# The last 256 tokens of the last projection, turned: tokens in the partitions instead of output channels

## The chip, the core and the metric

The kernel runs on one core of a Trainium2 chip. A core has a matrix engine (PE, with its weight loads shown as PEld), a vector engine (DVE), a scalar engine (ACT), GpSimd (POOL), and SyncE (SP), which here issues the DMA transfers. Each engine works through its own queue in order; they meet through semaphores. The metric is the device time of one execution in microseconds (us), the median over several runs.

## The reference, cut to what matters

Two layers over 1024 tokens of 1024 channels: one of attention, one of a gated recurrence. Each adds its result, times a gate per channel, to the residual stream. At the end stands an RMS norm per token. All of it is float32.

```python
def rmsnorm(x, g):
    x32 = x.astype(jnp.float32)
    y = x32 * lax.rsqrt(jnp.mean(x32 * x32, axis=-1, keepdims=True) + EPS)
    return (y * g.astype(jnp.float32)).astype(x.dtype)

# in rglru_mixer, layer 1: hs are the states of the recurrence
    y = jnp.transpose(hs, (1, 0, 2)).astype(h.dtype) * jax.nn.silu(gate)
    return y @ w_out
# in reference
        x = x + gate[:, None, :] * y
    return rmsnorm(x, final_g)
```

The change concerns `y @ w_out`, the gated addition and the final norm, for the last 256 of the 1024 tokens.

## The kernel before

Everything is kept with channels in the 128 partitions and tokens in the free dimension; a tensor of 1024 channels is 8 tiles (KT). A float32 product is made of three matmuls on rounded halves: the high half of the weight with the high half of the data, low with high, high with low (`gemm`, line 324). So one output tile of 128 channels takes 8 x 3 matmuls. All engine calls go through one recording helper, so nearly every row of the profile has line 85; rows are told apart by the names of their tiles.

Layer 1 runs in slots, one for each of 8 channel tiles (`slot`, and `last_slots` for the last two). In a slot ACT makes the gates, DVE scans over the tokens (`hs`), and the result, gated, is split into a high and a low half, `y1h` and `y1l`. Three engines share the splitting: ACT writes the high half, POOL or DVE subtracts for the low one.

The weights of the last projection, `wo1`, come in 8 output tiles of two halves each (`raw_wo`, 256 KB each) through three buffers of the pool `wp`, and are split into `wout`. The tile of output channels 0 (`whi_wo`, `wlo_wo`) stays in the small rotating buffers; tiles 1 to 4 and 5 to 7 (`wo`, by `split_out`) go into large ones that held the input of the layer before. A raw buffer is loaded again only when its split is done.

The last projection (from line 1609) has three stages of tokens: 0 to 511, 512 to 767, and 768 to 1023. In each, PE makes 8 output tiles. Of the first four tiles of the first stage PE does the first seven of eight channel tiles ahead, since the last slot's states come late. `residual` (DVE) multiplies by the gate column `mod` and adds `x`, which was read back from DRAM (`x1d`); ACT squares, DVE adds the squares up in `sqa`. PE sums over the partitions with a column of ones (`psq_n`), DVE and ACT make the root, two or four transposes spread the factor over the partitions (`rs_n`), and DVE and POOL multiply (`end_norm`). These sums run while the next stage is already on PE: its steps are put between matmuls through the list `pending`.

Matmuls stay in the order in which they are written (`ordered` holds "pe" there). In layer 1 all engines do, up to the end of the first stage of the projection; from there on a scheduler places what is not on PE, and it may place such work before earlier calls of the same engine. The order that it made can be read from the built program.

Of the kernel before, what the change touches and what calls it, by code (L numbers as in the profile page):

```python
# [12 lines left out]
F32 = mybir.dt.float32  # L13
F32R = mybir.dt.float32r
AF = mybir.ActivationFunctionType
ALU = mybir.AluOpType
# [27 lines left out]
def r32(ap):  # L44
    return ap.bitcast(F32)
# [3 lines left out]
def hybrid_trunk(  # L49
# [17 lines left out]
    maskrow: bass.AP,  # L67
    sinks: bass.AP,
    b_f: bass.AP,
    outT: bass.AP,  # L70
):
    nc = tc.nc
    ordered = set()
# [37 lines left out]

    def sub(eng, out, a, b):
        eng.tensor_tensor(out=out, in0=a, in1=b, op=ALU.subtract)

    const = ctx.enter_context(tc.tile_pool(name="const", bufs=1))
    wp = ctx.enter_context(tc.tile_pool(name="wp", bufs=1))
# [1237 lines left out]
    wout, wr = [], []  # L1354

    def split_out(e, engs=(gp, gp), parts=(0, 1)):

        n = e - 1
        if n % 4 == 0 and 0 in parts:
            wr[:] = [hl.tile([P, 4, KT, P], F32R, tag=f"hl{n // 4 * 2 + i}", name=f"wo1_{e}_{i}") for i in range(2)]  # L1360
        for c in parts:
# [162 lines left out]
    def last_slots(c):  # L1524

        w = ready.popleft()
        ps = gates(c)
        gate_s(c - 1, 1)  # L1530
        r, i_ = sig_ri(c, ps)
        split_r(c + 1)
        gate_a(c - 1, 0)
        split_next()
        th, a_, a2 = rt("th", c), rt("a", c), rt("a2", c)
        act.activation(th, r, AF.Tanh, scale=sp[:, c : c + 1])
        mul(dve, i_, i_, xcs[c])
# [16 lines left out]
        split_next()  # L1554
        wout.append(ready.popleft())
# [40 lines left out]
    norms = []  # L1596

    def end_norm(xn, psq, t0, tw):
        h, o = t0 // HALF, t0 % HALF
        for e in range(KT):  # L1600
            act.activation(xn[:, e], xn[:, e], AF.Copy, scale=col[:, C_FG + e : C_FG + e + 1])
        rs, prs = rstd_of(psq, tw, xp, ("vb", "rsb"), f"n2_{t0}")()
        for e in range(KT):
            mul(*((gp, xn[:, e], xn[:, e], rs) if e % 4 == 3 else (dve, xn[:, e], xn[:, e], prs[:, :tw])))
            if e % 2:
                sync.dma_start(outT[:, h, e - 1 : e + 1, o : o + tw], xn[:, e - 1 : e + 1])

    for t0, tw in ((0, 512), (512, 256), (768, 256)):
        h, o = t0 // HALF, t0 % HALF
        ts = slice(t0, t0 + tw)  # L1610
        xn = xp.tile([P, KT, tw], F32, tag="xn", name=f"x2_{t0}")
# [4 lines left out]
        for e in range(KT):  # L1616
# [18 lines left out]
            for e_, w_, ps in late_:  # L1635
                if t0 == 0 and e_ < AHEAD:
                    gemm(ps[:, :tw], w_, y1h[:, :, ts], y1l[:, :, ts], range(last, KT), first=False)
                residual(xn[:, e_], ps[:, :tw], 1, e_)
                if t0 < 768 or e_ + 1 < KT:
                    square_sum(sqa, xn[:, e_], e_, xp, f"o1_{t0}")  # L1640
            late_ = []
        ordered.clear()
        ordered.add("pe")
        sqs = [sqa]
        if t0 == 768:
            sqs.append(xp.tile([P, tw], F32, tag="sq", name=f"sq7_{t0}", bufs=2))
            act.activation(sqs[1], xn[:, KT - 1], AF.Square)
        psq, steps = sum_steps(sqs, tw, f"n2_{t0}")
        norms.append((xn, psq, t0, tw, steps))
        if t0 < 768:  # L1650
            continue
        for f in steps:
            f()
        end_norm(*norms.pop()[:4])


def _buckets(n):
# [7 lines left out]
def layouts(inputs):  # L1665
# [10 lines left out]
    def colv(v):  # L1676
# [30 lines left out]
        "maskrow": mask,  # L1707
        "sinks": f["attn_sinks"][0],
        "b_f": f["attn_b_f"][0],
    }  # L1710
    return {k: np.ascontiguousarray(v) for k, v in arrays.items()}

# [17 lines left out]
```

## Time and profile before

| | us |
|---|---|
| median of 3 runs | 873.88 (873.17 to 874.44) |
| the profiled execution | 874.64 |
| its span, first to last instruction | 872.8 |
| last matmul of the projection ends | 862.04 |
| first store of the last stage is issued | 867.39 |

PE is busy 98% of the span at a mean granted clock of 0.992. Between the span and the time of the execution lie 1.84 us that the trace doesn't show. A profile is of one execution; durations in it are for one instruction from start to end, and instructions of one engine overlap a little, so what a row of instructions costs is read from the distance of their starts.

### The profile page before, as it was taken

To read this page: it belongs to the slowest core of one execution; us is meant where nothing else is said; L and a number is where in the kernel's file an instruction comes from. 1 tells how busy PE (TensorE), PEld (TensorE's weight loads), DVE (VectorE), ACT (ScalarE), POOL (GpSimd) and SP (SyncE) were. 2 spreads that over 40 slices of the span, in tenths; PEclk is the share of its full clock that TensorE was granted. 3 is DMA by queue.
4 is the path that set the end of the run, shared out by engine and by line. 5 is a ranking of instruction groups with operands and counts; after the bars stand their busy time and mean duration, and the time that the engine had idled before them with its cause. 6 is when DMAs were issued, how large, how long until landed. Compare 5 with 4: busy or idle time off the path is not lost.

```text
span 872.8 us, 13447 instructions
## 1 busy us (share of the span) xinstructions
PE 854.9 (98%) x4618; PEld 728.4 (83%) x4618; DVE 567.6 (65%) x1121; ACT 535.8 (61%) x1047; POOL 382.1 (44%) x418
## 2 busy tenths in 40 slices
PE   9999999999999999999999999999999999999995
PEld 8888798888888888888888888878888877787995
DVE  6876567688677466566665668466676555973644
ACT  5756124688776565566766657457678666964632
POOL 3843132333343232232475564633755566875001
PEclk8999999999999999999999999999999999999998
DMA  9943772100113223333364464421212112226042
GB/s 344 403 168 132 221 231 86 43 25 25 37 44 115 88 79 125 89 92 119 100 200 151 157 206 169 133 78 61 80 55 72 55 60 74 97 90 212 1 145 97
DMA packets 54620, 103.83 MB, mean 119 GB/s; under 512 B 6960, under 2 KB 20720, under 8 KB 54040
## 3 DMA queue, kind: packets, MB, share of 16 engines
q1 hardware_dynamic: 53400, 101.93, 35.3%
q10 hardware_dynamic: 1152, 1.05, 0.5%
q8 instruction: 36, 0.59, 0.3%
q14 instruction: 32, 0.26, 0.1%
HBM read 94.02 MB, written 8.93 MB: 118 GB/s over the span
## 4 chain that ended last, share of the span: by engine, by line
PE 81%; DVE 5%; POOL 5%; issue 4%; ACT 3%; DMA 1%; SPq 0%; DVEq 0%; POOLq 0%; ACTq 0%
PE ps_fill L85 23%; PE pst L85 10%; PE ps_o L85 8%; PE ps_lx L85 6%; PE ps_o0c L85 5%; PE ps_lg L85 5%; PE oB L85 4%; PE ptB L85 3%; PE sB L85 3%; PE ps_v L85 3%; PE sA L85 2%; PE oA L85 2%; PE ptA L85 1%; POOL wo L85 1%; POOL wlo_lx L85 1%
## 5 line engine op out<-in xcount | busy, mean ns | idle before, releaser
L85 DVE TENSOR_TENSOR ptl_B<-ptB,pth_B 128x512 fp32r<-128x512 f32 (+1 forms) x80 | 50.9, 636 | 44.2 <-ACT pth_B L85 43.7
L85 PE MATMUL ps_o<-y1h,wo 128*128 128x256 f32 (+1 forms) x336 | 76.2, 320 | 0.7 <-POOL wo L85 0.7
L85 ACT ACTIVATE pB<-pB,mnB 128x128 f32<-128x128 f32 (+3 forms) x64 | 49.6, 775 | 32.2 <-DVE mnB L85 31.5
L85 ACT ACTIVATE pth_B<-ptB 128x512 fp32r<-128x512 f32 (+1 forms) x80 | 44.0, 552 | 33.6 <-PE ptB L85 33.3
L85 DVE SCALAR_TENSOR_TENSOR xc_r<-ps_lx,col,xc_r 128x509 f32<-128x509 f32 (+2 forms) x48 | 35.6, 744 | 43.4 <-ACT xt_r L85 42.2
L85 PEld LDWEIGHTS ps_o<-y1h,wo 128*128 128x128 f32 x336 | 56.1, 190 | 5.4 <-POOL wo L85 1.1
L85 POOL TENSOR_SCALAR_AFFINE_SELECT pB<-pB 128x128 f32<-128x128 f32 x64 | 18.8, 295 | 94.7 <-DMA pB<-gd 82.2
L85 PE MATMUL pst<-hh,ws 128*128 128x512 f32 x192 | 55.4, 397 | 0.0
L85 PE MATMUL ps_o<-y1l,wo 128*128 128x256 f32 (+1 forms) x168 | 53.6, 319 | 0.0
L85 PE MATMUL ps_lg<-h1h,wlo_lg 128*128 128x512 f32 x128 | 50.2, 392 | 0.9 <-POOL wlo_lg L85 0.8
L85 PE MATMUL ps_lx<-h1l,whi_lx 128*128 128x512 f32 x128 | 50.3, 393 | 0.2 <-POOL h1l L85 0.2
L85 PE MATMUL ps_lx<-h1h,wlo_lx 128*128 128x512 f32 x128 | 50.3, 393 | 0.1
L85 PE MATMUL ps_lx<-h1h,whi_lx 128*128 128x512 f32 x128 | 50.3, 393 | 0.0
L85 PE MATMUL ps_lg<-h1l,whi_lg 128*128 128x512 f32 x128 | 49.9, 390 | 0.0
L85 PE MATMUL ps_lg<-h1h,whi_lg 128*128 128x512 f32 x128 | 49.9, 389 | 0.0
L85 POOL TENSOR_TENSOR wlo_lx<-raw_lx,whi_lx 128x512 fp32r<-128x512 f32 x16 | 30.6, 1929 | 43.3 <-ACT whi_lx L85 26.8
L85 ACT ACT_TABLE_LOAD x35 | 44.9, 1283 | 5.1 <-issue 3.0
L85 PE MATMUL ptB<-ident,pB 128*128 128x128 f32 x288 | 45.3, 273 | 2.1 <-ACT pB L85 1.6
L85 PEld LDWEIGHTS ptB<-ident,pB 128*128 128x128 f32 x288 | 35.7, 140 | 12.8 <-ACT pB L85 2.8
L85 DVE CUSTOM_DVE_ANT_0 pB<-sB,pB 128x384 f32<-128x384 f32 (+2 forms) x64 | 35.1, 553 | 14.6 <-PE sB L85 8.1
L85 PEld LDWEIGHTS pst<-hh,ws 128*128 128x128 f32 x192 | 36.1, 189 | 8.7 <-issue 0.6
L85 ACT ACTIVATE pA<-pA,mnA 128x256 f32<-128x256 f32 (+1 forms) x64 | 31.2, 488 | 10.8 <-DVE mnA L85 10.5
(313 smaller groups left out, 2827.7 us busy)
## 6 DMA issues: line engine op xcount, KB each, us to landing
ada<-in_ada_dram SPq DMA_DIRECT2D x32, 512.0 KB
x<-in_xT_dram SPq DMA_DIRECT2D x20, 256.0 KB
ada<-in_ada_dram SPq DMA_DIRECT2D x4, 1024.0 KB
pB<-gd SPq DMA_DIRECT2D x8, 512.0 KB
raw_o0a<-in_wo_dram SPq DMA_DIRECT2D x16, 256.0 KB
raw_o0c<-in_wo_dram SPq DMA_DIRECT2D x16, 256.0 KB
x1d<-x SPq DMA_DIRECT2D x16, 256.0 KB
raw_lx<-in_wl_dram SPq DMA_DIRECT2D x16, 256.0 KB
```

What stands on the lines that cost most here:

```text
L85: ins = issue(*args, **kw)
```

## The change

The first two stages stay as they are. For the last 256 tokens the roles of the two operands are exchanged: 128 tokens of the gated states are loaded as weights, and the projection's weights move, 512 output channels at a time. The result has tokens in the partitions. So:

- the sum of squares of a token lies along the free dimension: ACT sums while it squares (`accum_out`), and the norm factor is one number per partition, with no matmul of ones and no spreading;
- the gate and the final factor `final_g` now vary along the free dimension and are needed as rows in all partitions: `grow` comes from the gate columns through DRAM (`dgate`) and a broadcast load, `gfrow` from a new input;
- the residual must be turned too: the last 256 columns of `x1d` are loaded at once (`xl`, shown as x_768) and turned by 16 transposes on PE, put behind matmuls of tile 5 of the second stage, and copied out by ACT (`x1t`);
- to have four output tiles side by side, the weights of output tile 0 are copied behind tile 7 in the large buffers (four copies on ACT), so the outputs stand in the order of tiles 1 to 7, 0;
- tokens 768 to 895 are done in two parts of 512 outputs, tokens 896 to 1023 in three (512, 256, 256); the output array has a second layout for them, which the host undoes.

```diff
+    def x1_steps():
+        def step(b, g, i, box=[]):
+            if i == 0:
+                box[:] = [(ps_s, ps_t)[g](f"x1t_{b}_{g}")]
+            tp(box[0][:, i * P : (i + 1) * P], xl[:, (4 * g + i + 1) % KT, b * P : (b + 1) * P])
+            if i == 3:
+                copy(x1t[:, b, 512 * g : 512 * g + 512], box[0])
+        return [lambda b=b, g=g, i=i: step(b, g, i) for b in range(2) for g in range(2) for i in range(4)]
 
-    for t0, tw in ((0, 512), (512, 256), (768, 256)):
+    for t0, tw in ((0, 512), (512, 256)):
...
+            if t0 and e == 5:
+                pending.extend(x1_steps())
...
+        if t0 == 0:
+            for c in range(2):
+                for i in range(2):
+                    copy(wrs_out[1][i][:, 3, 4 * c : 4 * c + 4], r32(w0[c][i]))
+            dgate = dram.tile([KT, P], F32, name="dgate")
+            sync.dma_start(dgate[0 : KT - 1].rearrange("e p -> p e"), mod[:, 1, 17:24])
+            sync.dma_start(dgate[KT - 1 : KT].rearrange("e p -> p e"), mod[:, 1, 16:17])
+            grow, gfrow = (xp.tile([P, S], F32, tag=n, name=n, bufs=1) for n in ("grow", "gfrow"))
+            sync.dma_start(grow, dgate.rearrange("e p -> (e p)").partition_broadcast(P))
+            sync.dma_start(gfrow, fgrow.partition_broadcast(P))
+            xl = xp.tile([P, KT, 256], F32, tag="xl", name="x2_768", bufs=1)
+            sync.dma_start(xl, x1d[:, 1, :, 256:512])
+            x1t = xp.tile([P, 2, S], F32, tag="x1t", name="x1t", bufs=1)
...
+    for b in range(2):
+        tok = slice(768 + b * P, 768 + (b + 1) * P)
+        u, xo = xl.rearrange("p (b e) t -> p b (e t)", b=2)[:, b], x1t[:, b]
+        ss = xp.tile([P, 8], F32, tag="ss", name=f"ss_{b}")
+        parts = ((0, 512), (512, 512)) if b == 0 else ((0, 512), (512, 256), (768, 256))
+        for i, (o, w) in enumerate(parts):
+            hi, lo = (t[:, o % 512 // P : (o % 512 + w) // P] for t in wrs_out[o // 512])
+            ps = ps_1(f"ps_t_{b}_{i}")
+            out = ps[:, :w].rearrange("p (e c) -> p e c", c=P)
+            if norms and i == 1:
+                end_norm(*norms.pop()[:4])
+            for k in range(KT):
+                if norms and k == 2:
+                    pending.extend(norms[0][4])
+                for n, (y, wgt) in enumerate(((y1h, hi), (y1h, lo), (y1l, hi))):
+                    mm(out, y[:, k, tok], wgt[:, :, k], start=(k == 0 and n == 0), stop=(k + 1 == KT and n == 2))
+                    if pending:
+                        pending.popleft()()
+            cs = slice(o, o + w)
+            mul(dve, u[:, cs], ps[:, :w], grow[:, cs])
+            add(dve, u[:, cs], u[:, cs], x1t[:, b, cs])
+            sq = xp.tile([P, 512], F32, tag="sq", name=f"sqt_{b}_{i}", bufs=2)
+            act.activation(sq[:, :w], u[:, cs], AF.Square, accum_out=ss[:, i : i + 1])
+            mul(dve, xo[:, cs], u[:, cs], gfrow[:, cs])
...
+        act.activation(xo[:, 0:512], xo[:, 0:512], AF.Copy, scale=y)
+        sync.dma_start(outM[b, :, 0:512], xo[:, 0:512])
+        dve.tensor_scalar(out=xo[:, 512:1024], in0=xo[:, 512:1024], scalar1=y, scalar2=None, op0=ALU.mult)
+        sync.dma_start(outM[b, :, 512:1024], xo[:, 512:1024])
```

Since the scheduler places the new work, the built program's order tells more than the diff. Three places follow; what is written to stands left of the arrow.

ACT in the last slot of layer 1, before: `a_r` is the decay and its square, `th_r` the square root that the scan's input needs, `wo` the high halves of the weight tiles.

```order
L85 ACTIVATE a_r_8160<-r_r_8153,nsp 128x1024
L85 ACTIVATE a_r_8161<-a_r_8160 128x1024
L85 ACTIVATE wo_1_0_8171<-raw_wo_2_1_8175 128x512
L85 ACT_TABLE_LOAD
L85 ACTIVATE th_r_8159<-th_r_8159,tiny 128x1024
L85 ACTIVATE wo_1_0_8171<-raw_wo_3_0_8179 128x512
```

The same place with the change:

```order
L86 ACTIVATE a_r_8160<-r_r_8153,nsp 128x1024
L86 ACTIVATE a_r_8161<-a_r_8160 128x1024
L86 ACTIVATE wo_1_0_8171<-raw_wo_2_1_8175 128x512
L86 ACTIVATE wo_5_0_8263<-whi_wo_0_0_8075 128x512
L86 ACTIVATE wo_5_0_8263<-whi_wo_0_1_8081 128x512
L86 ACTIVATE wo_5_1_8264<-wlo_wo_0_0_8076 128x512
L86 ACTIVATE wo_5_1_8264<-wlo_wo_0_1_8082 128x512
L86 ACT_TABLE_LOAD
L86 ACTIVATE th_r_8159<-th_r_8159,tiny 128x1024
L86 ACTIVATE wo_1_0_8171<-raw_wo_3_0_8179 128x512
```

The four copies of tile 0's weights, written behind the first stage, stand ahead of the last slot's square root.

SP's transfers from the last halves of tile 5 on, before (`x_0`, `x_512` and `x_768` are the residual of the three stages):

```order
L85 DMA raw_wo_5_0_8207<-in_wo_dram 128x512
L85 DMA x_0_8226<-x1d 128x512 x8
L85 DMA raw_wo_5_1_8238<-in_wo_dram 128x512
L85 DMA raw_wo_6_0_8242<-in_wo_dram 128x512
L85 DMA raw_wo_6_1_8267<-in_wo_dram 128x512
L85 DMA x_512_8495<-x1d 128x256 x8
L85 DMA raw_wo_7_0_8271<-in_wo_dram 128x512
L85 DMA raw_wo_7_1_8294<-in_wo_dram 128x512
```

With the change:

```order
L86 DMA raw_wo_5_0_8207<-in_wo_dram 128x512
L86 DMA dgate<-mod 128x7x1
L86 DMA x_0_8226<-x1d 128x512 x8
L86 DMA raw_wo_5_1_8238<-in_wo_dram 128x512
L86 DMA raw_wo_6_0_8242<-in_wo_dram 128x512
L86 DMA raw_wo_6_1_8267<-in_wo_dram 128x512
L86 DMA grow<-dgate 128x1024
L86 DMA gfrow<-in_fgrow_dram 128x1024
L86 DMA x_768_8506<-x1d 128x8x256
L86 DMA x_512_8509<-x1d 128x256 x7
L86 DMA raw_wo_7_0_8271<-in_wo_dram 128x512
L86 DMA x_512_8509<-x1d 128x256
```

The last half, `raw_wo_7_1`, is the next row. The store of the gate columns stands ahead of the first stage's residual, and the two broadcast rows and the whole of `x_768` ahead of the last weight tile. Transfers take turns on eight completion semaphores; by this turn the issue of `raw_wo_7_0` now also waits until `x_768` has landed, where before it waited for the first `x_512`.

PE in tile 5 of the second stage, with the change; before, the matmuls of `ps_o` followed each other:

```order
L86 MATMUL ps_o_512_5_8702<-y1h,wo_5_0_8263 128x256
L86 MATMUL x1t_0_8704<-ident,x_768_8506 128x128
L86 MATMUL ps_o_512_5_8702<-y1h,wo_5_1_8264 128x256
L86 MATMUL x1t_0_8704<-ident,x_768_8506 128x128
L86 MATMUL ps_o_512_5_8702<-y1l,wo_5_0_8263 128x256
L86 MATMUL x1t_0_8704<-ident,x_768_8506 128x128
```

A transpose stands behind each of the first 16 of the 24 matmuls.

More of the change, by code (lines that the diff above doesn't have):

```diff
@@ L69, in hybrid_trunk @@
     b_f: bass.AP,
-    outT: bass.AP,
+    fgrow: bass.AP,
+    out: bass.AP,
 ):
@@ L113, in sub @@
         eng.tensor_tensor(out=out, in0=a, in1=b, op=ALU.subtract)
+    cut = D * (S - 256)
+    outT = out[0:cut].rearrange("(p k t) -> p k t", p=P, k=KT)
+    outM = out[cut:].rearrange("(b p c) -> b p c", p=P, c=D)
     const = ctx.enter_context(tc.tile_pool(name="const", bufs=1))
@@ L1352, in split_next @@
         ready.append(w)
-    wout, wr = [], []
+    wout, wr, w0, wrs_out = [], [], [], []
     def split_out(e, engs=(gp, gp), parts=(0, 1)):
@@ L1553, in last_slots @@
         w = ready.popleft()
-        split_next()
-        wout.append(ready.popleft())
+        for _ in range(2):
+            raw, name = raws.popleft()
+            w0.append(split_raw(raw, [P, 4, P], name))
+            load_next()
+        wout.append([tuple(t[:, k % 4] for t in w0[k // 4]) for k in range(KT)])
         c += 1
@@ L1638, in hybrid_trunk @@
                 residual(xn[:, e_], ps[:, :tw], 1, e_)
-                if t0 < 768 or e_ + 1 < KT:
-                    square_sum(sqa, xn[:, e_], e_, xp, f"o1_{t0}")
+                square_sum(sqa, xn[:, e_], e_, xp, f"o1_{t0}")
             late_ = []
@@ L1643, in hybrid_trunk @@
         ordered.add("pe")
[L1644 to L1648, printed above, removed]
-        norms.append((xn, psq, t0, tw, steps))
[L1650 to L1654, printed above, removed]
+        psq, steps = sum_steps(sqa, tw, f"n2_{t0}")
+        norms.append((xn, psq, t0, tw, steps))
@@ new lines, in hybrid_trunk @@
+    for b in range(2):
[22 more added lines that the diff above has]
+            mul(dve, xo[:, cs], u[:, cs], gfrow[:, cs])
+        n = len(parts)
+        v, y, t = (ss[:, i : i + 1] for i in (4, 5, 6))
+        if n == 3:
+            add(dve, ss[:, 0:1], ss[:, 0:1], ss[:, 1:2])
+        dve.tensor_scalar(out=v, in0=ss[:, 0:1], scalar1=1.0 / D, scalar2=EPS, op0=ALU.mult, op1=ALU.add)
+        dve.scalar_tensor_tensor(out=v, in0=ss[:, n - 1 : n], scalar=1.0 / D, in1=v, op0=ALU.mult, op1=ALU.add)
+        act.activation(y, v, AF.Sqrt)
+        dve.reciprocal(y, y)
+        dve.scalar_tensor_tensor(out=t, in0=v, scalar=-0.5, in1=y, op0=ALU.mult, op1=ALU.mult)
+        mul(dve, t, t, y)
+        dve.scalar_tensor_tensor(out=y, in0=t, scalar=1.5, in1=y, op0=ALU.add, op1=ALU.mult)
+        act.activation(xo[:, 0:512], xo[:, 0:512], AF.Copy, scale=y)
+        sync.dma_start(outM[b, :, 0:512], xo[:, 0:512])
+        dve.tensor_scalar(out=xo[:, 512:1024], in0=xo[:, 512:1024], scalar1=y, scalar2=None, op0=ALU.mult)
+        sync.dma_start(outM[b, :, 512:1024], xo[:, 512:1024])
@@ L1709, in layouts @@
         "b_f": f["attn_b_f"][0],
+        "fgrow": np.roll(f["final_g"], -P),
     }
@@ L1723 @@
     ]
-    out = nc.dram_tensor("out_0_dram", (P, 2, KT, HALF), F32, kind="ExternalOutput").ap()
+    out = nc.dram_tensor("out_0_dram", (S * D,), F32, kind="ExternalOutput").ap()
     with tile.TileContext(nc, schedule_with_timeline_sim=True) as tc:
@@ L1728 @@
     got = r.results[0]["out_0_dram"]
-    return np.ascontiguousarray(got.transpose(1, 3, 2, 0).reshape(1, S, D))
+    cut = D * (S - 256)
+    first = got[:cut].reshape(P, KT, S - 256).transpose(2, 1, 0).reshape(S - 256, D)
+    last = np.roll(got[cut:].reshape(256, D), P, axis=1)
+    return np.ascontiguousarray(np.concatenate([first, last]).reshape(1, S, D))
```

6 lines of the change are left out of this document (3 added, 3 removed).

## The prediction

> **What bounds the kernel now.** I read the page first, then the stretches from the last projection on, then the chain of waits backwards from the end, then the timelines of single engines around the places that the chain names.
>
> ```profile
> span 872.8 us, 13447 instructions
> PE 854.9 (98%) x4618; PEld 728.4 (83%) x4618; DVE 567.6 (65%) x1121; ACT 535.8 (61%) x1047; POOL 382.1 (44%) x418
> 792.00:819.60 27.60, 27.43 (x144) 23.70 (x145) 10.21 (x15) 13.57 (x21) 8.93 (x8) 1.00 0.36 125
> 819.60:862.10 42.50, 42.50 (x359) 42.50 (x358) 20.36 (x53) 16.09 (x35) 4.01 (x4) 1.00 0.29 100
> 862.10:872.80 10.70, 1.53 (x9) 0.98 (x8) 3.80 (x13) 1.48 (x4) 1.41 (x2) 0.64 0.29 98
> ```
>
> The page says that PE is busy for 98% of the span. The stretches say what that means here: in the projection of the first 512 tokens (792.0 to 819.6) and of the two quarters behind it (819.6 to 862.1) PE has next to no gap; in the last 10.7 us it has almost nothing to do. So there are two ways to change the time: what PE is given or has to wait for before 862.1, and the tail behind it.
>
> ```profile
> 790.83 1.30 POOL wo L85
> ...
> 792.17 27.70 PE ps_o L85 x144
> 792.17 0.50 PE L85 MATMUL ps_o<-y1h,wo 128*128 128x512 f32 x1 [0.68 <-POOL wo L85]
> ```
>
> The chain of waits reaches PE at 792.17 from POOL, and PE's own row agrees: it idled 0.68 us for the low half of a weight tile (output tile 4). Up to this row the end is set by POOL, ACT and DVE; behind it PE runs without a wait to the tail. Whatever is put into the chain ahead of 792.17 goes through in full.
>
> **The change, part by part.** *Matmuls (A).* Removed are 8 x 24 matmuls of 256 columns. Added are 24 x 3 of 512 columns and 24 x 2 of 256.
>
> ```profile
> 813.83 0.28 PE L85 MATMUL ps_o<-y1h,whi_wo 128*128 128x256 f32 x1
> 813.95 0.28 PE L85 MATMUL ps_o<-y1h,wlo_wo 128*128 128x256 f32 x1
> ...
> 819.71 0.28 PE L85 MATMUL psq_n<-ones,sqa 128*128 128x2 f32 x2
> ```
>
> Two matmuls of 256 columns start 0.12 us apart (813.83, 813.95). The stretch 792.0 to 819.6 holds 144 matmuls, 96 of 512 columns and 48 of 256: (27.6 - 48 x 0.12) / 96 = 0.2275 us for one of 512. So 192 x 0.12 = 23.0 us become 72 x 0.2275 + 48 x 0.12 = 22.1: **-0.9 us**. Roles are swapped but each still has one 128x128 load beside it, so I add nothing for it.
>
> *Sixteen transposes of the residual (B)*, one behind each matmul of tile 5 of the second stage.
>
> ```profile
> 850.14 0.38 PE L85 MATMUL rs_n<-ident,vb_n 128*128 128x128 f32 x2
> ...
> 850.59 0.28 PE L85 MATMUL ps_o<-y1l,wo 128*128 128x256 f32 x1
> 844.05 0.28 PE L85 MATMUL psq_n<-ones,sqa 128*128 128x2 f32 x2
> ...
> 844.74 0.40 PE L85 MATMUL ps_o<-y1h,wo 128*128 128x256 f32 x2
> ```
>
> The two transposes at 850.14 put the third matmul behind them at 850.59, where 0.24 us of matmuls alone would have put it at 850.38: 0.105 us each, issued together. The two sums at 844.05 stand alternately with matmuls: from 844.05 to 844.74 are 0.69 us with two matmuls (0.24) in it, so 0.225 each, but each of these takes two passes. The new transposes alternate, with one pass: between 1.7 and 3.6 us for 16, and I take 0.15 each, **+2.4 us**. None of it is covered, since PE has no gap there.
>
> *Four weight copies on ACT (C).* The weights of tile 0 are copied beside those of tiles 5 to 7. The order puts the four copies of 128x512 ahead of the table load and the square root of the last recurrent slot.
>
> ```profile
> 775.27 0.61 ACT L85 ACTIVATE wo<-raw_wo 128x512 fp32r<-128x512 f32 x1
> 775.90 1.28 ACT L85 ACT_TABLE_LOAD   x1
> 777.20 1.15 ACT L85 ACTIVATE th_r<-th_r,tiny 128x1024 f32<-128x1024 f32 x1
> ...
> 789.60 0.63 ACT L85 ACTIVATE y1h<-sg_r 128x512 fp32r<-128x512 f32 x1 [1.96 <-DVE sg_r L85]
> 790.13 1.66 ACT L85 ACTIVATE wo<-raw_wo 128x512 fp32r<-128x512 f32 x3
> 778.38 1.23 DVE L85 TENSOR_TENSOR i_r<-i_r,th_r 128x1024 f32<-128x1024 f32 x1 [1.76 <-ACT th_r L85]
> ```
>
> Today the copy at 775.27 is followed at once by the table load (775.90) and the square root (777.20); DVE waits 1.76 us for that square root (778.38), then come the scan, the gating, the last split of y (ACT 789.60, which waits for DVE), and only behind it in ACT's queue the copy of the weight tile (790.13) whose POOL half PE awaits at 792.17. Three such copies take 1.66 us, so four take **2.2 us**, and no link of that chain has room: PE gets its tile at 794.4. The buffers that the copies write were last read by the gate projection of the second half, long done, so the copies themselves wait for nothing. If ACT had been idle there, this would cost nothing; it is not.
>
> *Loads moved ahead of the last weights (D).* This is the largest term. On SP's queue five new transfers stand ahead of the two halves of the last weight tile.
>
> ```profile
> SPq L85 <- DVE mod L85: 3.1, 1, 3.1
> 787.51 3.65 SPq L85 DMA_DIRECT2D x<-x1d  x8
> 792.14 2.81 SPq L85 DMA_DIRECT2D raw_wo<-in_wo_dram  x3
> 795.01 3.84 SPq L85 DMA_DIRECT2D x<-x1d  x8
> 798.95 1.56 SPq L85 DMA_DIRECT2D raw_wo<-in_wo_dram  x2
> 788.50:795.00 6.50, 5.82 (x26) 4.50 (x25) 3.08 (x4) 2.19 (x4) 4.29 (x4) 1.00 0.97 323
> 795.00:797.00 2.00, 2.00 (x10) 1.66 (x9) 0.00 (x0) 0.10 (x1) 0.00 (x0) 1.00 1.00 345
> 797.00:800.60 3.60, 3.60 (x17) 2.98 (x17) 0.00 (x0) 1.79 (x3) 2.99 (x3) 1.00 0.87 291
> 803.12 1.28 ACT L85 ACTIVATE wo<-raw_wo 128x512 fp32r<-128x512 f32 x2 [3.95 <-DMA raw_wo<-in_wo_dram]
> 804.31 0.61 ACT L85 ACTIVATE sqa<-x 128x512 f32<-128x512 f32 x1
> ```
>
> Now: SP is held by the last modulation row (3.1 us), issues the eight loads of x for the first stage at 787.51, three weight halves, the eight small loads of the second stage, and the last two halves from 798.95. The DMA engines are 97% busy from 788.5 to 795.0 at 323 GB/s (this is the 2.1 MB of x) and do 291 GB/s with the 1 KB pieces of the second stage. ACT waits for the last halves until 803.12. With the change the 2.2 us of (C) delay the modulation row; the store of seven gate columns comes first (its 896 pieces of 4 bytes have no like here: at least one more issue, 3.65 / 8 = 0.46 us; at most what as many 1 KB pieces take, 896 KB at 291 GB/s = 3.2 us; I take 0.5, since almost no bytes move); then two broadcast rows (1.05 MB in 4 KB pieces; nearest are the 345 GB/s of 795 to 797, mostly 2 KB pieces: 3.0 us) and the third quarter of x1 at once (1.05 MB in 1 KB pieces at 291 GB/s: 3.6 us). The engines are already full, so these 6.6 us don't overlap with anything. The last two halves land about 2.2 + 0.5 + 6.6 = **9.3 us later**, near 812.4.
>
> The Trainium skill (DMA: Bandwidth & Descriptors, Specifications) gives 512 bytes as the smallest transfer for full rate, below which the engine reads, modifies and writes. No run here shows what that does to 4-byte stores; by it the 0.5 would grow, which is the third rival below.
>
> Who waits for these halves: PE at the first low matmul of tile 7, and ACT, whose queue has all the squares of the first stage behind the two copies.
>
> ```profile
> 810.95 0.74 DVE L85 SCALAR_TENSOR_TENSOR x<-ps_o,mod,x 128x512 f32<-128x512 f32 x1
> ...
> 818.54 0.69 DVE L85 TENSOR_TENSOR sqa<-sqa,sq_o 128x512 f32<-128x512 f32 x1 [0.70 <-ACT sq_o L85]
> ```
>
> ACT's first square starts at 804.31, right behind the last copy. From there ACT and DVE run as a chain, one output tile per 2.05 us: DVE takes tile 4 at 810.95 and adds the last square at 818.54, done 819.23. PE wants that sum at 819.71: 0.48 us of room. PE also wants at 813.83 the bank that DVE frees at 811.69: 2.1 us of room. Moved by 9.3, the sum is there at 828.5 instead of 819.23, so the sum of squares on PE starts 9.3 - 0.5 = **8.8 us later** than now. The 2.2 us of (C) are inside this; the rest shows as three more idle times of PE: at tile 7 (about 3 us), at the first tile of the second stage (about 2, waiting for DVE's bank) and at the sums (about 1.6).
>
> *The tail (E).* Removed: sums on PE, the spreading by two transposes, eight multiplications and four stores of 256 KB. Added: a chain per partition.
>
> ```profile
> 862.06 0.50 DVE x L85
> ...
> 863.69 0.18 DVE psq_n L85
> ...
> 864.93 0.43 DVE vb_n L85
> ...
> 866.61 0.42 DVE x L85
> 867.39 1.98 SPq L85 DMA_DIRECT2D out_dram<-x  x4
> L85 ACT ACTIVATION_READ_ACCUMULATOR pA<-pA,mnA 128x1 f32 x64 | 12.0, 188 | 0.0
> 814.44 0.72 ACT L85 ACTIVATE x<-x,col 128x512 f32<-128x512 f32 x1
> ```
>
> Now from the last matmul (862.04) to the first store (867.39) are 5.35 us, and to the end of the span (872.8) 5.41 more, in which 1.05 MB move. After: multiply 0.42 and add 0.42 on DVE, square 0.42 and its accumulator 0.19 on ACT, six tiny steps (863.69 to 864.93 are six: 1.24), one scaling of 128x512 (0.72 on ACT, DVE's half beside it), with hand-overs of 0.02 to 0.04: 3.5 us. Then half the bytes: 0.52 MB at 291 GB/s are 1.8 us less, 3.6 us. 10.76 become 7.1: **-3.6 us**. The first 128 of these tokens (DVE about 4.6 us of work under the next 5.5 us of matmuls) and the norm of the second quarter lie under PE. That norm's sums come six matmuls of 512 columns into the new part (1.4 us plus one) while they need about 1.4 us of DVE and ACT: a near miss, 0 to 0.3.
>
> Sum: +8.8 (C and D) - 0.9 (A) + 2.4 (B) - 3.6 (E) = **+6.7 us**. The profiled execution took 874.64 with its span of 872.8, and the runs' median is 873.88; on the span this gives 879.5, on the median **880.6**.
>
> **The rivals.** *1: the loads are hidden.* If the last halves came no more than about 2 us later than now, D would vanish into the chain's room and only C remained: 2.2 - 0.9 + 2.4 - 3.6 = +0.1, 874.0, and the lower end of B makes it 873.3. For it: the two halves need only be split by 805 and 806 for PE. Against it: the 97% row, and the fact that the issue of the first of them now also waits for the landing of the new 1 MB load (they share a completion semaphore). It decides where PE starts tile 7: before 811 it holds. This is the side that is not slower.
>
> *2: the gain of the tail is smaller.* If ACT's accumulating square or the small steps cost double and the 2 KB pieces of the store go no faster per DMA, E falls from 3.6 to about 1.8, and the time is 882.4. For it: the trace shows this chain only with eight columns. It stays on the same side.
>
> *3: the small store is slow.* If each 4-byte piece costs a read and a write of what a 1 KB piece costs now (64 pieces per engine in 3.6 us, so 0.056 us each; 56 pieces x 2 x 0.056 = 6.3 us), everything in D moves by 5.8 us more: 886.4. For it: nothing in the trace but the missing of such a row; against it: the pieces may be in flight together. The rule of the Trainium skill named above is this mechanism.
>
> *4: the order is not kept by the chip,* so that the change only does what its words say: -0.9 + 2.4 - 3.6 = -2.1, 871.8. Every row above shows engines and queues taking instructions in the listed order, so I give it little.
>
> **How the numbers follow.** The sum as it stands, with its own range 877.5 (faster broadcasts, transposes at 0.105) to 884 (transposes at 0.225, loads at 261 to 291 GB/s): 0.62. Rival 1: 0.14, of which its lower end, 0.04, would be measured as faster and 0.10 as no change. Rival 2: 0.08. Rival 3: 0.12. Rival 4: 0.04. A change under 0.2% (1.75 us) can't be told from none. Faster: 0.04 + 0.04 (rival 4) = 0.08; the same: 0.10; slower: the rest, 0.82. The range has to leave out no more than 0.2: from 873.5, where only the lower part of rival 1 (0.05) and rival 4 (0.04) lie below, to 886.0, with about half of rival 3 (0.06) above.
>
> **What would show it.** Right: four copies between 775 and 778 on ACT, the square root near 779.4; PE's wait for POOL ending at 794.4 and no longer 792.17; ACT's wait for the last weight half ending between 810 and 813; PE idle before the first tile of the second stage, ended by DVE; the span's tail near 7.1 us behind the last matmul. Wrong: PE without gaps between 795 and 830, the last halves landed by 806, or a tail of over 9 us. The forecast fails most likely on D, since it is one chain of transfers whose rate I take from neighbours.

## Result: 888.9 us, slower by more than twice the forecast

The changed kernel takes **888.9 us** (median of 4 runs, 887.5 to 890.0) against 873.6 us before, run on the same chip (873.2 to 874.4): a ratio of **1.0169, 95% interval 1.0157 to 1.0181**. The forecast was 880.6 us with a range up to 886.0. The sign was right and the size was not: +15.3 us in place of +6.7.

The page of the changed kernel, its first lines:

```profile
span 886.9 us, 13303 instructions
PE 859.4 (97%) x4552; PEld 726.1 (82%) x4552; DVE 569.8 (64%) x1125; ACT 537.7 (61%) x1051; POOL 382.1 (43%) x416
```

TensorE is now busy for 859.4 us (854.9 before) of a span that grew by 14.1 us (872.8 before). So part of the growth, 9.6 us, is idle time, and part is work at a lower clock, as the stretches below show. SP's own timeline of the changed kernel says where it begins (start, time until the last of the row was issued, count):

```profile
789.01 0.38 SPq L86 DMA_DIRECT2D dgate<-mod  x1
789.43 12.95 SPq L86 DMA_DIRECT2D x<-x1d  x8
802.48 2.46 SPq L86 DMA_DIRECT2D raw_wo<-in_wo_dram  x3
805.21 0.33 SPq L86 DMA_DIRECT2D grow<-dgate  x1
805.89 0.33 SPq L86 DMA_DIRECT2D gfrow<-in_fgrow_dram  x1
806.56 6.30 SPq L86 DMA_DIRECT2D x<-x1d  x8
...
817.87 0.38 SPq L86 DMA_DIRECT2D raw_wo<-in_wo_dram  x1
```

Behind the store of the gate columns (789.01) the eight loads of x need **12.95 us** to be issued; before, the same row took 3.65. The stretches of the changed kernel (length, busy time of PE, PEld, DVE, ACT and POOL with counts, granted clock of TensorE, busy share of the DMA engines, GB/s) show what moved meanwhile:

```profile
791.00:802.00 11.00, 8.81 (x31) 6.87 (x32) 0.80 (x2) 2.19 (x4) 3.76 (x3) 0.84 0.42 32
804.00:808.50 4.50, 0.00 (x0) 0.00 (x0) 0.41 (x1) 0.00 (x0) 0.00 (x0) 0.96 1.05 401
808.50:814.00 5.50, 4.16 (x9) 2.97 (x10) 0.00 (x0) 1.89 (x3) 3.74 (x3) 0.50 1.05 381
822.00:838.00 16.00, 13.38 (x87) 11.92 (x88) 10.56 (x17) 11.91 (x21) 1.33 (x2) 1.00 0.00 1
838.00:879.80 41.80, 41.76 (x285) 38.35 (x283) 22.57 (x57) 13.43 (x31) 4.46 (x4) 1.00 0.25 89
879.80:886.90 7.10, 0.00 (x0) 0.00 (x0) 2.56 (x9) 1.43 (x4) 0.00 (x0) 0.74 0.20 74
```

For 11 us, from 791 to 802, the queue moves 32 GB/s, where before it moved 323 (788.5 to 795). Then 401 GB/s: the rows, x and the weights rush in, late. TensorE stands still from 804 to 808.5 and works at half clock (0.50) from 808.5 to 814. The tail behind the last matmul is 7.1 us, as forecast. The waits of TensorE, DVE and ACT in the timelines of the changed kernel:

```profile
792.34 0.51 PE L86 MATMUL ps_o<-y1h,wo 128*128 128x512 f32 x1 [1.64 <-ACT wo L86]
793.69 0.50 PE L86 MATMUL ps_o<-y1h,wo 128*128 128x512 f32 x1 [0.85 <-POOL wo L86]
809.28 0.79 PE L86 MATMUL ps_o<-y1h,wo 128*128 128x512 f32 x1 [5.77 <-ACT wo L86]
...
828.70 0.39 PE L86 MATMUL ps_o<-y1h,whi_wo 128*128 128x256 f32 x1 [1.07 <-DVE x L86]
836.25 0.38 PE L86 MATMUL psq_n<-ones,sqa 128*128 128x2 f32 x2 [1.42 <-DVE sqa L86]
802.50 0.75 DVE L86 SCALAR_TENSOR_TENSOR x<-ps_o,mod,x 128x512 f32<-128x512 f32 x1 [10.01 <-DMA x<-x1d]
808.60 1.99 ACT L86 ACTIVATE wo<-raw_wo 128x512 fp32r<-128x512 f32 x3 [15.27 <-DMA raw_wo<-in_wo_dram]
...
821.12 0.63 ACT L86 ACTIVATE wo<-raw_wo 128x512 fp32r<-128x512 f32 x1 [0.39 <-DMA raw_wo<-in_wo_dram]
```

DVE's first residual waits 10.01 us for x; ACT waits 15.27 us for a weight half that is queued behind x; TensorE then waits 5.77 us for ACT. ACT takes the last weight half at 821.12 (forecast: near 812.4), and the sums of squares start at 836.25, 16.5 us later than before (819.71), where 8.8 were forecast.

### The profile page after: what moved, and what is told of

Same layout as the page of the kernel before. It is cut to its first block, busy times and chain, and to the rows that moved or that the text cites. A ratio compares the mean times of both kernels' runs of the same rounds, so it can differ in the third digit from the quotient of the medians.

```text
span 886.9 us, 13303 instructions
## 1 busy us (share of the span) xinstructions
PE 859.4 (97%) x4552; PEld 726.1 (82%) x4552; DVE 569.8 (64%) x1125; ACT 537.7 (61%) x1051; POOL 382.1 (43%) x416
## 3 DMA queue, kind: packets, MB, share of 16 engines
q10 hardware_dynamic: 1152, 1.05, 0.4%
## 4 chain that ended last, share of the span: by engine, by line
PE 72%; DMA 8%; DVE 7%; ACT 6%; issue 3%; POOL 3%; SPq 1%; POOLq 0%; DVEq 0%; ACTq 0%
PE ps_fill L86 23%; PE ps_lx L86 6%; PE ps_lg L86 6%; PE pst L86 5%; PE ps_o0c L86 5%; PE oB L86 4%; PE ptB L86 3%; PE sB L86 3%; DMA x<-x1d 3%; PE ps_v L86 3%; PE ps_t L86 3%; DMA ada<-in_ada_dram 2%; PE ps_o L86 2%; PE sA L86 2%; PE oA L86 2%
## 5 line engine op out<-in xcount | busy, mean ns | idle before, releaser
L86 PE MATMUL ps_o<-y1h,wo 128*128 128x512 f32 (+1 forms) x224 | 60.8, 359 | 9.7 <-ACT wo L86 7.4
L86 PEld LDWEIGHTS ps_o<-y1h,wo 128*128 128x128 f32 x224 | 40.7, 197 | 16.9 <-ACT wo L86 8.6
L86 DVE CUSTOM_DVE_ANT_0 pB<-sB,pB 128x384 f32<-128x384 f32 (+2 forms) x64 | 35.1, 553 | 14.8 <-PE sB L86 8.5
L86 PE MATMUL ps_o<-y1l,wo 128*128 128x512 f32 (+1 forms) x112 | 39.5, 353 | 0.0
```

Of the source, the lines that this page charges most:

```text
L86: ins = issue(*args, **kw)
```

## The experiments

Three theories stood after the result. **1**: the store in 4-byte pieces holds the queue for 11 to 12 us. **2**: the moved loads (two rows, the third quarter of x1) cost far more than forecast. **3**: the copies on ScalarE and the halved clock do it. Times of the kernel before, run beside these, were 873.8 to 874.2 us in the median; differences below are taken against those of the same runs.

**The change without the store.**

```diff
-sync.dma_start(dgate[0 : KT - 1].rearrange("e p -> p e"), mod[:, 1, 17:24])
-sync.dma_start(dgate[KT - 1 : KT].rearrange("e p -> p e"), mod[:, 1, 16:17])
-sync.dma_start(grow, dgate.rearrange("e p -> (e p)").partition_broadcast(P))
+sync.dma_start(grow, fgrow.partition_broadcast(P))
```

> The changed kernel without the store of the gate columns; the gate row is loaded from the row of final factors instead, so the gate of the last 256 tokens is wrong, while every other transfer and instruction stays. Theory 1 (the 896 pieces of 4 bytes hold the queue for 11 to 12 us, and that is what the forecast lacked): the first residual's data comes about 11 us earlier, the last weight half about 9 us earlier, the time falls to 878 to 881. Theory 2 (the two broadcast rows and the third quarter of x1 ahead of the last weights cost far more than forecast): 886 to 889, nearly as with the store. Theory 3 (the copies on ScalarE and the halved TensorE clock behind the two long idle times are the cause): 885 to 889 if the clock still halves.

Measured: **879.3 us** (879.2 to 880.0), ratio 1.0065 (1.0050 to 1.0080). Theory 1 holds: without two small stores the kernel is 9.6 us faster (10.1, if each is taken against the kernel before in its own runs), and stands 1.3 us from the forecast that had given the store 0.5 us. In this run SP issues the eight loads of x in 3.65 us again, and ScalarE takes the last weight half at 811.75:

```profile
788.50 3.65 SPq L86 DMA_DIRECT2D x<-x1d  x8
...
811.75 0.63 ACT L86 ACTIVATE wo<-raw_wo 128x512 fp32r<-128x512 f32 x1 [0.32 <-DMA raw_wo<-in_wo_dram]
```

The forecast had said near 812.4. So the chain of transfers without the store goes about as worked out.

**The store alone, in the kernel before.**

```diff
         norms.append((xn, psq, t0, tw, steps))
+        if t0 == 0:
+            dgate = dram.tile([KT, P], F32, name="dgate")
+            sync.dma_start(dgate[0 : KT - 1].rearrange("e p -> p e"), mod[:, 1, 17:24])
+            sync.dma_start(dgate[KT - 1 : KT].rearrange("e p -> p e"), mod[:, 1, 16:17])
```

> The kernel before with nothing added but the store of the gate columns, at the place in SP's queue where the change has it (ahead of the eight loads of x1 for the first 512 tokens). Nothing reads what it writes. Theory 1: the eight loads come 11 to 12 us later, the last weight halves land near 812 instead of 803, and the time is 881 to 885. Theory 2 and 3: the store costs under 1 us of the queue, 873.5 to 875.

Measured: **883.7 us** (883.1 to 884.4), ratio 1.0113 (1.0100 to 1.0126), +9.6 us. Its SP timeline, and the row at which ScalarE takes the last weight half:

```profile
787.27 0.38 SPq L85 DMA_DIRECT2D dgate<-mod  x1
787.70 12.12 SPq L85 DMA_DIRECT2D x<-x1d  x8
...
813.20 0.63 ACT L85 ACTIVATE wo<-raw_wo 128x512 fp32r<-128x512 f32 x1 [1.44 <-DMA raw_wo<-in_wo_dram]
```

A store of 3.5 KB, whose result nobody reads, costs as much in the one kernel as in the other: x needs 12.12 us, the last half is taken at 813.20, where before the last two are taken one right behind the other from 803.12. The other part of the store, one column of 0.5 KB, goes out at 622.70 here (622.31 in the change), as its column is ready by then. Nothing is seen of a delay by it: the seven columns are issued at 787.27, and before, the loads of x at 787.51. This settles theory 1 from both sides; theories 2 and 3 can be responsible for what is left only.

**All five transfers behind the last weight half** (the block keeps them in the order of the code on SP, the one after it the copies on ScalarE).

```diff
+with paced("sync"):
     dgate = dram.tile([KT, P], F32, name="dgate")
     sync.dma_start(dgate[0 : KT - 1].rearrange("e p -> p e"), mod[:, 1, 17:24])
...
     sync.dma_start(xl, x1d[:, 1, :, 256:512])
```

> The changed kernel with all five transfers (store, two rows, third quarter of x1) kept behind the last weight half in SP's queue; nothing is left out. Theory 1 and 2 alike: the store still takes its 11 to 12 us, but nothing of the projection waits behind it; left are the matmuls (-0.9), the transposes (+1.9 by their spacing in the changed kernel), the copies on ScalarE (+1.5 to 2) and the tail (-3.6): -1.1 to -0.6, so 872.5 to 873.1. Theory 3: the delay by the copies and the halved clock stay, 880 or more.

Measured: 881.0 us with a wide spread (875.2 to 883.1), ratio 1.0072 (1.0046 to 1.0098). That is 8 us above what theory 1 had said. Rows of SP, then ScalarE, then TensorE:

```profile
801.16 1.59 SPq L86 DMA_DIRECT2D raw_wo<-in_wo_dram  x2
802.79 1.84 SPq L86 DMA_DIRECT2D dgate<-mod  x2
...
811.57 0.63 ACT L86 ACTIVATE wo<-raw_wo 128x512 fp32r<-128x512 f32 x1 [5.59 <-DMA raw_wo<-in_wo_dram]
818.95 0.39 PE L86 MATMUL ps_o<-y1h,whi_wo 128*128 128x256 f32 x1 [2.01 <-DVE x L86]
```

The store is issued right behind the last weight half, and the half is there only at 811.6. What the DMA engines move in this run from 801 to 813, in slices of 0.3 us:

```profile
GB/s 318 314 311 225 307 266 300 212 171 212 219 191 128 39 24 1 0 0 0 0 0 0 0 0 0 0 0 0 0 0 0 0 0 0 0 0 0 0 0 0
```

Loads, weights and store move side by side up to 805.8; from there until the half is taken no byte is recorded. So what stands just ahead of the store comes late too, and not because its bytes are slow. What it waits for in these 5 us the trace doesn't show. The expectation was wrong in taking "behind" for "out of the way".

Two stretches of the same run, the first around a pause of TensorE of 2.01 us that ends at 818.95, the second around one of 1.41 us that ends at 826.49:

```profile
816.00:820.00 4.00, 1.99 (x14) 1.49 (x12) 2.61 (x5) 2.61 (x5) 0.00 (x0) 1.00 1.02 331
826.00:831.00 5.00, 4.51 (x25) 4.52 (x26) 2.44 (x9) 3.66 (x7) 0.00 (x0) 0.66 0.01 3
```

Behind the longer pause TensorE keeps its full clock (1.00, and so on up to 827); behind the shorter one it falls to half (0.50 from 828 to 830).

**The same, and the four copies behind the first stage's squares.**

```diff
+with paced("act"):
     for c in range(2):
         for i in range(2):
             copy(wrs_out[1][i][:, 3, 4 * c : 4 * c + 4], r32(w0[c][i]))
```

> As the one with the five transfers kept behind the last weight half, and the four weight copies kept behind the squares of the first 512 tokens in ScalarE's queue as well; nothing is left out. If the copies ahead of the square root cost what the chain of waits says (C, 1.5 to 2.2 us), the time is that much lower than with them in front: 870.5 to 871.5. If they were hidden, both times agree within 0.3 us.

Measured: **877.0 us** (875.0 to 878.3), ratio 1.0034 (1.0022 to 1.0046). The copies do cost something, but the time isn't the 871 expected, for the same reason as above: the last weight half is taken at 807.72. TensorE's one longer wait, in its timeline:

```profile
815.09 0.39 PE L86 MATMUL ps_o<-y1h,whi_wo 128*128 128x256 f32 x1 [2.08 <-DVE x L86]
```

The stretch behind that wait, at half clock (0.52):

```profile
816.00:819.00 3.00, 3.00 (x17) 3.00 (x16) 2.31 (x4) 1.80 (x3) 0.00 (x0) 0.52 0.81 280
```

**A store in rows of 512 bytes, away from the weights.** TensorE turns the eight columns into eight rows, behind a matmul of tile 1 of the second stage; the four copies stay late as above.

```diff
+def gate_rows():
+    pg = ps_s("dg")[0:KT, 0:P]
+    tp(pg, mod[:, 1, 16:24])
+    copy(grt, pg)
+    sync.dma_start(dgate[0 : KT - 1], grt[1:KT])
+    sync.dma_start(dgate[KT - 1 : KT], grt[0:1])
+    sync.dma_start(grow, dgate.rearrange("e p -> (e p)").partition_broadcast(P))
+with paced("sync"):
+    sync.dma_start(gfrow, fgrow.partition_broadcast(P))
...
+    sync.dma_start(xl, x1d[:, 1, :, 256:512])
...
+            if t0 and e == 1:
+                pending.append(gate_rows)
```

> Nothing is left out. The eight gate columns are turned into eight rows by one more matmul on TensorE, behind a matmul of tile 1 of the second stage, copied by ScalarE and stored in 8 pieces of 512 bytes; the row of final factors and the third quarter of x1 stand behind the last weight half, the gate row behind the new store, the four weight copies behind the squares of the first 512 tokens. Theory 1 (the store's pieces of 4 bytes delayed the last weight half even from behind it, which is why moving the transfers back did not bring the time to 871): the last weight half lands as in the kernel before, near 803, TensorE has no wait for VectorE ahead of the second stage, and the time is 870.5 to 871.8 (-0.9 + 1.9 - 3.6 + 0.1 for the new transposition). Rival (the two broadcasts and the third quarter of x1 disturb the last half even from behind): it lands at 805 or later and the time stays at 875 to 877.

Measured: **872.0 us** (870.3 to 872.2), ratio **0.9964 (0.9952 to 0.9977)**: this version is faster than the kernel before by 0.2 to 0.5%. Its waits of TensorE from 785 on (one row), ScalarE's first square and the new store, from its timelines:

```profile
791.95 0.50 PE L86 MATMUL ps_o<-y1h,wo 128*128 128x512 f32 x1 [0.69 <-POOL wo L86]
804.28 0.61 ACT L86 ACTIVATE sqa<-x 128x512 f32<-128x512 f32 x1
821.36 0.58 SPq L86 DMA_DIRECT2D dgate<-grt  x2
822.82 0.34 SPq L86 DMA_DIRECT2D grow<-dgate  x1
```

And in its chain of waits (start, us, engine, tile, count):

```profile
791.95 24.82 PE ps_o L86 x120
```

TensorE has no wait left but the 0.69 us that the kernel before has too, and ScalarE's first square stands at 804.28 (804.31 before); so the other transfers behind the last weight half don't hold it up. The gate row can be loaded 1.5 us after its store began.

**The same with the copies in front**, as in the change (the block around the copies is taken away again).

> As the one with wide store and late loads, but the four weight copies stay ahead of the square root as in the change; nothing is left out. Forecast of C: TensorE gets tile 4 1.5 to 2.2 us later, time 872.5 to 873.5. With the halved clock that followed the two waits at 792 and 793 in the changed kernel (50% from 794 to 797.6) another 1.6 to 1.8 us: 874 to 875.3. If C was hidden: the same as with late copies.

Measured: **874.4 us** (11 runs, 872.9 to 875.7), ratio 1.0003 (0.9994 to 1.0012). So the copies in front cost 2.4 us by the medians, 3.4 by the ratios. TensorE's waits in its timeline:

```profile
791.94 0.50 PE L86 MATMUL ps_o<-y1h,wo 128*128 128x512 f32 x1 [1.62 <-ACT wo L86]
793.29 0.50 PE L86 MATMUL ps_o<-y1h,wo 128*128 128x512 f32 x1 [0.85 <-POOL wo L86]
```

The row of its chain of waits that answers to the one above:

```profile
793.29 26.41 PE ps_o L86 x120
```

And a stretch right behind the second wait:

```profile
794.00:797.00 3.00, 3.00 (x9) 2.32 (x8) 0.00 (x0) 0.00 (x0) 1.71 (x2) 0.50 1.03 381
```

The tile comes 1.34 us later in these two profiled executions (793.29 against 791.95), and the same 120 matmuls take 26.41 us in place of 24.82, since TensorE runs at half clock from 794 to 797. Together 2.9, against 2.8 between the two spans (873.0 and 870.2).

**The narrow store, but late.** DVE copies the gate columns behind its last addition of the first stage, and the store reads that copy.

```diff
+with paced("dve"), paced("sync"):
+    dve.tensor_copy(gcol, mod[:, 1, 16:24])
+    sync.dma_start(dgate[0 : KT - 1].rearrange("e p -> p e"), gcol[:, 1:KT])
+    sync.dma_start(dgate[KT - 1 : KT].rearrange("e p -> p e"), gcol[:, 0:1])
+    sync.dma_start(grow, dgate.rearrange("e p -> (e p)").partition_broadcast(P))
```

> Nothing is left out. The store keeps its 896 pieces of 4 bytes, but reads a copy of the columns that VectorE makes behind its last addition of the first stage, so that it starts near 820, when no weight is under way; the other loads and the copies stand as in the kernel with wide store and late loads. If the pieces cost only what is queued near them, the time equals that of the wide store, 870.5 to 871.8, though the store still takes about 10 us. If they cost something wherever they stand: 875 or more.

Measured: **871.8 us** (871.1 to 871.9), ratio 0.9965 (0.9952 to 0.9979), the same as with rows of 512 bytes. SP's timeline:

```profile
819.33 0.98 SPq L86 DMA_DIRECT2D dgate<-gcol  x2
830.24 0.33 SPq L86 DMA_DIRECT2D grow<-dgate  x1
```

The load behind the store waits from 820.3 to 830.2, about 10 us. The stores of finished tokens behind it go out at 830.67 (829.32 with the wide store), and the kernel ends no later for it (span 870.1 us, 870.2 with the wide store). So the store costs what is queued around it. Of the 10 us the trace shows the DMA engines at work only from about 820.0 to 821.5; behind that they rest, but for fetches of instructions, until the load is issued.

**What the 10 us depend on.** Four other stores in the kernel before, at the same place, that nobody reads. Twice the columns:

```diff
-sync.dma_start(dgate[0 : KT - 1].rearrange("e p -> p e"), mod[:, 1, 17:24])
-sync.dma_start(dgate[KT - 1 : KT].rearrange("e p -> p e"), mod[:, 1, 16:17])
+sync.dma_start(dgate[0 : 2 * KT - 2].rearrange("e p -> p e"), mod[:, 1, 10:24])
+sync.dma_start(dgate[2 * KT - 1 : 2 * KT].rearrange("e p -> p e"), mod[:, 1, 9:10])
```

> The kernel before with twice the store: 14 columns, 1792 pieces of 4 bytes, at the same place. If the price is per piece (theory 1), the eight loads wait twice as long, about 24 us instead of 12, and the time rises by about 20 us to 893 to 897; if it is a fixed delay of such a transfer, the time stays at 883 to 885.

Measured: 890.5 us, ratio 1.0182 (1.0164 to 1.0201), between the two expectations. This run has a second delay in it: its second store, of one column, was ready early and went out among the loads of the modulation weights, at this row of its SP timeline:

```profile
123.52 0.42 SPq L85 DMA_DIRECT2D dgate<-mod  x1
```

From 150 us on the engines are some 5 us later than in the run with seven columns. (The next expectation puts it near 105 us; it is 123.5.) Hence the repetition without it:

```diff
-sync.dma_start(dgate[2 * KT - 1 : 2 * KT].rearrange("e p -> p e"), mod[:, 1, 9:10])
```

> The kernel before with 14 columns (1792 pieces of 4 bytes) at the place of the seven, and without the second store of one column that the run with twice the store had put among the loads near 105 us. If the delay is fixed, or set by the pieces of one 512-byte row and not by their sum: 883 to 886. If it is a price per piece: 892 to 895.

Measured: 884.9 us (883.7 to 885.2), ratio 1.0124 (1.0104 to 1.0144): twice the pieces, 11.1 us in place of 9.6. No price per piece. The other way, one column only:

```diff
-sync.dma_start(dgate[0 : 2 * KT - 2].rearrange("e p -> p e"), mod[:, 1, 10:24])
+sync.dma_start(dgate[0:1].rearrange("e p -> p e"), mod[:, 1, 23:24])
```

> The kernel before with a store of one column (128 pieces of 4 bytes into 512 bytes that lie together) at the place of the seven; nothing reads it. Price per piece: a seventh of the 9.6 us that seven columns cost, 875 to 876. Fixed delay of such a store: the eight loads of x1 wait as with seven columns, 882 to 884.

Measured: 882.0 us (880.9 to 883.0), ratio 1.0094 (1.0074 to 1.0114): a seventh of the pieces, and 8.2 us of the 9.6 are still there. Last, the seven columns to a wider target, each piece 512 bytes from the next:

```diff
-dgate = dram.tile([KT, P], F32, name="dgate")
-sync.dma_start(dgate[0:1].rearrange("e p -> p e"), mod[:, 1, 23:24])
+dgate = dram.tile([KT - 1, P, 128], F32, name="dgate")
+sync.dma_start(dgate[:, :, 0].rearrange("e p -> p e"), mod[:, 1, 17:24])
```

> The kernel before with the store of the seven columns, but each of the 896 pieces of 4 bytes goes to an address of its own, 512 bytes from the next; nothing reads it. If the delay comes from many pieces that write into the same 512 bytes of memory and wait for one another, it is gone: 873.5 to 876. If it comes from the pieces being small: 882 to 885, as with the seven columns.

Measured: 874.9 us (874.3 to 877.7), ratio 1.0017 (1.0007 to 1.0027): as many pieces, as small, and 1.1 us. The loads of x behind each of the three stores, in the order one column, seven columns to addresses 512 bytes apart, fourteen columns:

```profile
786.23 10.84 SPq L85 DMA_DIRECT2D x<-x1d  x8
```

```profile
787.62 4.29 SPq L85 DMA_DIRECT2D x<-x1d  x8
```

```profile
787.67 12.50 SPq L85 DMA_DIRECT2D x<-x1d  x8
```

10.84, 4.29 and 12.50 us, where the kernel before needs 3.65 and seven columns 12.12. The source is the same seven columns as in the first store, and the pieces are as many and as small, so what costs is that the pieces lie side by side, 128 of them in one stretch of 512 bytes. More columns, so more such stretches, add little.

## Why the prediction was right and wrong

Each term by the runs that isolate it, in us:

| term | forecast | measured | from |
|---|---|---|---|
| A, B and E: matmuls, transposes, tail | -2.1 | -2.1 (-3.1) | wide store, all late, against before |
| C: four copies ahead of the square root | +2.2 | +2.4 (+3.4) | copies in front against late |
| D: rows and third quarter of x1 ahead of the last weights | +6.1 | +4.9 (+5.4) | change without the store (879.3) against loads late (874.4) |
| D: the store | +0.5 | +9.6 (+9.1) | change (888.9) against without the store (879.3) |
| sum | +6.7 | +14.8 (+14.8) | +15.3 seen |

(The forecast's 8.8 for C and D is split as it was worked out: 2.2, 0.5, the rest.) The first figure is the difference of medians, the one in brackets that of the ratios to the kernel before in the same runs; the two differ by up to 1 us, and no term is known better than that. The 0.5 us between the sum of medians and the result is the distance of the medians of before in the two sets of runs (873.6 and 874.2).

- **A, B and E: right, with B somewhat too dear.** The tail is 7.1 us (879.80 to 886.90) where 7.1 was forecast. In TensorE's timeline of the changed kernel the sixteen transposes stand between these rows, the first and the eighteenth matmul of tile 5:

```profile
846.18 0.28 PE L86 MATMUL ps_o<-y1h,wo 128*128 128x256 f32 x1
849.99 0.28 PE L86 MATMUL ps_o<-y1l,wo 128*128 128x256 f32 x1
```

That is 3.81 us with seventeen matmuls, 2.04 us at 0.12, so 1.8 us for B in place of 2.4 (0.11 each, nearer to the 0.105 of the two issued together than to the 0.15 taken). The last stage takes TensorE 23.0 us (856.58 to 879.60) in place of 23.7 (838.17 to 861.86), each with the norm of the second quarter in it: -0.7 for A in place of -0.9. With the tail this makes -2.5, against -2.1 and -3.1 in the table, whose version holds one more small transposition.
- **C: right in place, and in size partly by chance.** The four copies stand where forecast:

```profile
774.73 0.61 ACT L86 ACTIVATE wo<-raw_wo 128x512 fp32r<-128x512 f32 x1
775.25 1.14 ACT L86 ACTIVATE wo<-whi_wo 128x512 fp32r<-128x512 f32 x2
776.29 1.14 ACT L86 ACTIVATE wo<-wlo_wo 128x512 fp32r<-128x512 f32 x2
777.45 1.28 ACT L86 ACT_TABLE_LOAD   x1
778.74 1.15 ACT L86 ACTIVATE th_r<-th_r,tiny 128x1024 f32<-128x1024 f32 x1
```

From the copy of the raw weights to the square root are 4.01 us in ScalarE's timeline of the changed kernel, before 1.93: 2.1 us, forecast 2.2. TensorE's wait for POOL ends at 793.69 (forecast 794.4). What the forecast did not have is the halved clock behind it, 1.6 us for the matmuls between 793 and 820. In the two profiled executions compared above the delay of the tile was 1.3, as the one with late copies was 0.7 us later ahead of them. Over eight profiled executions that wait ends at 791.1 to 792.2 without copies in front (before, and three with late copies) and at 793.1 to 793.7 with them (the change and three others), 1.8 us apart in the mean. With the 1.6 us this makes 3.4, the figure in brackets; that the medians come so near to 2.2 is chance.
- **D, the moved loads: right, somewhat too dear.** The last half is taken at 811.75 without the store, forecast 812.4, and ScalarE's first square stands 8.0 us later than before (812.29, 804.31), where 9.3 were forecast with the store's 0.5; the price is 4.9 in place of 6.1.
- **D, the store: the step that failed.** The prediction put it as "at least one more issue, 0.46 us; at most what as many 1 KB pieces take, 3.2 us; I take 0.5, since almost no bytes move". Both ends were wrong: the upper bound priced a piece as an independent transfer, and 0.5 took bytes for the price. The runs show about 10 us for 128 pieces into one 512-byte row, hardly more for seven or fourteen rows at once. "The forecast fails most likely on D" was right, its reason (the rates of the loads) was not.
- **Rival 3** named the store and gave 886.4 us, near to 888.9, and got only a chance of 0.12. Its working does not hold, though: by 0.056 us for a read and a write each, one column would have cost 0.9 us and not 8.2, and 896 pieces to addresses of their own 6.3 us and not 1.1. The Trainium skill (DMA: Bandwidth & Descriptors, Specifications) says that below 512 bytes the engine reads, modifies and writes. The runs fit that rule if such writes to one 512-byte stretch wait for each other: 128 of them in about 10 us would be 0.08 us each, an estimate from the run with the late narrow store. That they do so is inferred from the four stores, and no trace row shows a single such write; the recorded work of the DMA engines ends long before the wait does.
- **Rivals 1, 2 and 4** fell: the loads were not hidden (874.4 with them late, 879.3 with them in front), the tail came in as forecast, and the chip kept the listed order.
- **The three idle times of TensorE** were forecast at tile 7 (about 3 us), ahead of the second stage (2) and at the sums (1.6); there are waits for DVE at 828.70 (1.07) and 836.25 (1.42) as said, and a larger one at 809.28 (5.77) that the store put there. Without the store they are 1.5 at tile 7 (0.65 and 0.84, ending at 811.49 and 812.84), 1.05 and 1.41: in the places forecast, and smaller. The sums start 7.2 us later than before there (826.94), where 8.8 were forecast, and part of these 7.2 is the halved clock.
- **The range** ended at 886.0 because half of rival 3 was left out. With a store whose like the trace does not hold, an upper bound taken from a row of other pieces was no bound.

## What to carry to other kernels

A store that writes one column, 4 bytes from each partition, into one contiguous row cost its queue 8 to 11 us here, however few bytes it held, and delayed what stood just ahead of it as well as what stood behind it; turn it into rows on TensorE first, or issue it where nothing is queued for 10 us. A transfer with no like in the trace is best bounded by a run of its own before any sum is built on it, and moving loads "behind" something means checking that the other transfer has landed. The change itself is worth 2 to 4 us (0.9964, 0.9952 to 0.9977) once its store, its loads and its copies stand where nobody waits.

## What the runs showed of the hardware

- **Small writes side by side in one row land late.** 128 pieces of 4 bytes into the same 512 bytes: +8.2 us; 896 into seven such rows: +9.6; 1792 into fourteen: +11.1; 896 pieces to addresses 512 bytes apart: +1.1. That the writes wait for each other is inferred. Whether the unit is 512 bytes or less, and whether it matters that the pieces come over several DMA engines, was not tried.
- **TensorE's clock can halve behind pauses of 1.4 to 2.1 us, and does not always.** Here a single pause of 2.08 us was followed by a clock of 0.52 from 816 to 819, and two of 1.62 and 0.85 us with one matmul of 0.50 us between them by 0.50 from 794 to 797, 1.6 us of loss. The Trainium skill (TensorE: Matmul & The Clock Gate, Part 1) gives an idle window of about 3.4 us, free-running, before half clock. The length of a pause alone does not decide it: with all five transfers late, one of 2.01 us was followed by full clock and one of 1.41 us by half clock, and in the changed kernel one of 1.42 us (836.25) was not followed by it (1.00 in the stretches from 822 to 879.8). The pause of 0.68 us of the kernel before was not followed by it either. What decides was not measured.
